# A feed-forward of two matrix products in blocks: written order on four engines, block loads one by one, and the first unit of the second product plain

## The chip, the cores and the metric

One core of a Trainium2 chip runs the kernel. TensorE multiplies (PE; its weight loads are PEld), VectorE works element by element (DVE), ScalarE copies, rounds and applies functions (ACT), GpSimd does a few small powers (POOL), and SyncE (SP) issues the loads from device memory. Each engine runs its own instructions strictly in the order in which they stand on it, and semaphores make one engine wait for another. The metric is the device time of one execution in microseconds (us).

## What is computed

A decoder layer for 256 rows of width 2048, in float32: three attention branches merged by gates, and then a feed-forward block. The change touches the feed-forward alone:

```python
h2 = _rms(x, g_ffn_norm[layer])
x = x + jnp.square(jax.nn.relu(h2 @ w_ff_in[layer])) @ w_ff_out[layer]
```

`w_ff_in` is 2048 x 8192 and `w_ff_out` 8192 x 2048. The kernel takes the 8192 hidden columns in four quarters q of 2048. Quarter by quarter the first product gives the hidden rows, which are squared, turned and kept in `hid`, and the second product adds its part to `x1`.

## The kernel before

**A weight tile.** TensorE multiplies in float32r, so each float32 operand is kept as a rounded part (`hi`) and a remainder (`lo`), and a product takes three passes: hi x hi, lo x hi, hi x lo. A weight tile comes by DMA (`raw`, 128 x 2 x 512), ScalarE casts it to `whi` (L189), and VectorE subtracts to get `wlo` (L190). `raw`, `whi` and `wlo` have four buffers each. `wahead` keeps the two entries behind the current one in preparation, in the order of `plan`.

**Plain strips.** `strip_rows` computes 512 output columns: eight steps of one weight tile, each with 12 matmuls of 128x512 for the two halves of the rows.

**Units.** All but the first quarter's first product goes by `unit`: 1024 columns in which 6 of the 16 row blocks of the weights are multiplied by a Strassen-Winograd scheme with seven products and the other ten steps ("n") are plain tiles. Four weight blocks of 128 x 3 x 512 (B11, B12, B21, B22, tile `sraw`, six buffers) are loaded, and VectorE makes four combinations of them in place or in a fresh buffer: T3 = B22 - B12 in B12's buffer (L211), T2 = B11 + T3 in a new buffer (L213), T1 = B22 - T2 in B11's (L216), T4 = B21 - T2 in T2's (L219). Each of the seven operands is cast and split in two pieces of two and one k-blocks (`SUBS`, written here a and b, as T3a and T3b; lines 263 and 264), with 6 and 3 matmuls. A unit has 10 x 12 + 7 x 9 = 183 matmuls; two plain strips for the same columns have 192. The order of the 24 entries is the list `UNIT`, and `UNIT_LATE` for the first unit of the second product:

```python
UNIT = _order("B11", "T2", "n", "n", "T3", "n", "T1", "n", "B21", "n", "T4", "n", "B22", "n", "n", "n", "n")
```

`early` folds the partial products together after T1 (p1s, uu, wz); `late` takes the finished accumulators of a column half: in the second product an addition to `x1` (L871), in the first product an addition (L846) and two functions on ScalarE (L847, L848), after which `hidden_rows` transposes the rows on TensorE, splits them into `hid`, and for two of the four column groups makes the sums `ss` that the second product's unit needs. These follow-up steps are generators; `pump` advances one step after each entry.

**What sets the order.** The whole program is scheduled when it is built: the code gives priorities, and a scheduler places the instructions of each engine, the DMAs on SP among them. So what stands on an engine can differ from what the code emits.

Of the kernel before, what the change touches and what calls it, by code (L numbers as in the profile page):

```python
# [11 lines left out]
F32 = mybir.dt.float32  # L12
# [42 lines left out]

UNIT = _order("B11", "T2", "n", "n", "T3", "n", "T1", "n", "B21", "n", "T4", "n", "B22", "n", "n", "n", "n")
UNIT_LATE = _order("n", "n", "n", "n", "n", "B11", "T2", "T3", "n", "T1", "n", "B21", "n", "T4", "B22", "n", "n")
UNIT_NORMAL = [(kg, c) for kg in range(SH, KT // GA) for c in range(2)]
# [22 lines left out]

def _units(mat, orders):

    w = mat.reshape(KT, P, -1, 2, 512)
    out = []
    for u, order in enumerate(orders):
        block = lambda kts, c: out.append(np.ascontiguousarray(w[kts, :, u, c].transpose(1, 0, 2)).reshape(-1))
        rest = iter(UNIT_NORMAL)
        for k in order:
            if k == "n":  # L90
                kg, c = next(rest)
                block([GA * kg + g for g in range(GA)], c)
            elif k == ("B11", 0):
                for kts, c in ((K1, 0), (K2, 1), (K1, 1), (K2, 0)):
                    block(kts, c)
    return np.concatenate(out)


@with_exitstack
def tile_block(ctx: ExitStack, tc: tile.TileContext, io):  # L100
# [56 lines left out]
    plan.extend([("w_out", GA, 512)] * (4 * KT // GA))  # L157
    def plan_units(name, orders=(UNIT, UNIT)):
        for order in orders:
            plan.extend((name, GA, 512) if k == "n" else (name, k) for k in order)  # L160

    for q in range(4):
        if q == 0:
            plan.extend([("w_ff_in", GA, 512)] * (4 * KT // GA))
            plan_units("w_ff_out", (UNIT_LATE, UNIT))
        else:
            plan_units("w_ff_in")
            plan_units("w_ff_out")
# [23 lines left out]

    blocks = {}

    def uload(name, which):

        def block():
            off = offs.get(name, 0)
            size = P * SH * 512
            offs[name] = off + size  # L200
            raw = pool[0].tile([P, SH, 512], F32, tag="sraw", name="sraw")
            last_load[0] = nc.sync.dma_start(
                raw, io[name][off:off + size].rearrange("(p g n) -> p g n", p=P, g=SH)).ins
            return raw

        b = blocks
# [61 lines left out]

    def unit(name, sums, xh, xl, early, late, order=UNIT):

# [17 lines left out]

        for what in order:
            if what == "n":  # L290
# [521 lines left out]
    def split_rows():  # L812
        yield
        for g, f in enumerate(scaled):
            yield
            split_into(x1T[:, 4 * g:4 * g + 4, 0, :], x1T[:, 4 * g:4 * g + 4, 1, :], f)
            if g < len(SUBS):
# [3 lines left out]
                        sx[:, :, :, g0:g0 + n, :])  # L821

    for q in range(4):
        hid = [ff.tile([P, 4, 2, S], F32R, tag="hid", name="hid", bufs=4) for _ in range(4)]
# [35 lines left out]
        hidl = lambda kt, t: hid[kt // 4][:, kt % 4, 1, t * P:(t + 1) * P]  # L860
        for u in range(2):
# [12 lines left out]

            unit("w_ff_out", sums_for(lambda kt, hl, ts: hid[kt // 4][:, kt % 4, hl, ts], ss), hidh, hidl, early, late,
                 UNIT_LATE if (q, u) == (0, 0) else UNIT)
        drain(attn, "x")
# [66 lines left out]
```

## Time and profile before

| what | value |
|---|---|
| median of three runs | 1409.28 us (1407.91 to 1409.47) |
| profiled execution: its own time, its span | 1414.6 us, 1412.8 us |
| busy: PE, DVE, ACT | 1394.9, 1039.5, 760.0 us |
| twelve units, second product of q = 0 (u = 1) up to the last unit's start | 526.02 us |
| in these twelve: DVE busy, PE waiting with a named releaser | 473.52 us, 8.2 us |

The profiled execution is 5.3 us above the median of the runs, and its own time is 1.8 us above its span (from the first to the last instruction). PE's busy share says little, since matmuls overlap and their ends are modelled; what tells is the time from one start to the next.

### The profile page before, as it was taken

The page shows a single profiled execution, that of the slowest core. Times are in us where ns is not written, and L with a number is a line of the kernel's source. Part 1 is how long each engine was busy: PE and PEld are TensorE (multiplying, and loading weights), DVE is VectorE, ACT ScalarE, POOL GpSimd, SP SyncE. Part 2 cuts the span into 40 slices and gives each one's busy share as a digit, 9 for nine tenths or more (in the row PEclk, how much of TensorE's full clock was granted, in tenths as well). Part 3 has the DMA queues.
Part 4 walks back from the last instruction along what each step waited for, and adds up shares of the span by engine and source line. Part 5 has one row for each costly group of instructions (what it writes and reads, how often), then busy time and mean ns, then how long its engine had stood idle before and what let it go on. Part 6 is the DMA issues. An engine that isn't in the chain of part 4 may idle for free. (4 is left out here: it accounts for less than half of the span.)

```text
span 1412.8 us, 17222 instructions
## 1 busy us (share of the span) xinstructions
PE 1394.9 (99%) x6334; PEld 1151.0 (81%) x6334; DVE 1039.5 (74%) x1185; ACT 760.0 (54%) x992; POOL 37.6 (3%) x41
## 2 busy tenths in 40 slices
PE   8999999999999999999999999999999999999998
PEld 6888888888888888888888887878888788887887
DVE  6657657566755646565567799988888989888896
ACT  6545545466444444445455655566545665456653
POOL 0211102000000000000000000000000000000000
PEclk9999999999999999999999999999999999999999
DMA  9647545665566666676665746555575555664552
GB/s 324 233 139 240 171 146 165 200 183 164 184 205 199 200 202 200 193 237 201 185 229 183 237 164 228 189 168 179 189 239 191 180 177 191 216 229 151 181 192 90
DMA packets 75236, 274.54 MB, mean 194 GB/s; under 512 B 8592, under 2 KB 9360, under 8 KB 74896
## 3 DMA queue, kind: packets, MB, share of 16 engines
q1 hardware_dynamic: 75008, 273.42, 59.7%
q8 instruction: 50, 0.82, 0.2%
q14 instruction: 34, 0.28, 0.1%
q10 hardware_dynamic: 144, 0.02, 0.0%
HBM read 271.31 MB, written 2.10 MB: 194 GB/s over the span
## 5 line engine op out<-in xcount | busy, mean ns | idle before, releaser
L190 DVE TENSOR_TENSOR wlo<-raw,whi 128x1024 fp32r<-128x1024 f32 (+2 forms) x419 | 501.0, 1204 | 270.6 <-ACT whi L189 260.6
L189 ACT CAST whi<-raw 128x1024 fp32r<-128x1024 f32 (+2 forms) x419 | 432.9, 1038 | 459.4 <-PE acc L253 295.0
L253 PE MATMUL acc<-whi,xT 128*128 128x512 f32 (+1 forms) x1472 | 394.1, 389 | 5.6 <-ACT xT L266 5.6
L253 PEld LDWEIGHTS acc<-whi,xT 128*128 128x128 f32 x1472 | 273.3, 189 | 61.1 <-ACT xT L266 6.3
L253 PE MATMUL acc<-wlo,xT 128*128 128x512 f32 (+1 forms) x736 | 227.1, 389 | 0.0
L263 ACT CAST whi<-sraw 128x1024 fp32r<-128x1024 f32 x196 | 161.8, 837 | 116.1 <-PE acc L280 85.0
L264 DVE TENSOR_TENSOR wlo<-sraw,whi 128x1024 fp32r<-128x1024 f32 x196 | 183.4, 952 | 33.7 <-PE acc L280 19.1
L280 PE MATMUL acc<-whi,hid 128*128 128x512 f32 x736 | 189.7, 390 | 0.0
L280 PEld LDWEIGHTS acc<-whi,hid 128*128 128x128 f32 x736 | 137.5, 188 | 28.2
L253 PEld LDWEIGHTS acc<-wlo,xT 128*128 128x128 f32 x736 | 137.3, 189 | 28.3 <-issue 1.0
L280 PE MATMUL acc<-whi,x1T 128*128 128x512 f32 x552 | 143.6, 396 | 0.0
L280 PEld LDWEIGHTS acc<-whi,x1T 128*128 128x128 f32 x552 | 104.8, 191 | 23.6 <-ACT whi L189 1.6
L280 PE MATMUL acc<-wlo,hid 128*128 128x512 f32 x368 | 102.4, 390 | 0.4 <-DVE wlo L190 0.4
L280 PE MATMUL acc<-wlo,x1T 128*128 128x512 f32 x276 | 77.9, 395 | 5.5 <-DVE wlo L264 5.5
L280 PEld LDWEIGHTS acc<-wlo,hid 128*128 128x128 f32 x368 | 68.7, 188 | 15.9 <-DVE wlo L190 1.8
L253 PE MATMUL acc<-whi,x1T 128*128 128x512 f32 x256 | 70.0, 393 | 0.0
L253 PE MATMUL acc<-whi,mT 128*128 128x512 f32 x256 | 69.9, 391 | 0.0
L280 PEld LDWEIGHTS acc<-wlo,x1T 128*128 128x128 f32 x276 | 51.9, 190 | 18.2 <-DVE wlo L264 6.8
L253 PE MATMUL acc<-whi,oT 128*128 128x512 f32 x224 | 60.0, 390 | 0.6 <-ACT oT L266 0.6
L253 PEld LDWEIGHTS acc<-whi,mT 128*128 128x128 f32 x256 | 47.9, 188 | 9.6
L253 PEld LDWEIGHTS acc<-whi,x1T 128*128 128x128 f32 x256 | 47.5, 188 | 9.4
L253 PEld LDWEIGHTS acc<-whi,oT 128*128 128x128 f32 x224 | 42.0, 188 | 9.5 <-ACT oT L266 0.9
(196 smaller groups left out, 1273.8 us busy)
## 6 DMA issues: line engine op xcount, KB each, us to landing
raw<-in_w_gate_dram SPq DMA_DIRECT2D x96, 512.0 KB, 3.5
raw<-in_w_ff_in_dram SPq DMA_DIRECT2D x92, 512.0 KB, 4.3
raw<-in_w_ff_out_dram SPq DMA_DIRECT2D x80, 512.0 KB, 4.5
raw<-in_w_proj_dram SPq DMA_DIRECT2D x77, 512.0 KB, 3.9
sraw<-in_w_ff_out_dram SPq DMA_DIRECT2D x32, 768.0 KB, 5.4
sraw<-in_w_ff_in_dram SPq DMA_DIRECT2D x24, 768.0 KB, 4.2
raw<-in_w_out_dram SPq DMA_DIRECT2D x32, 512.0 KB, 3.5
raw<-in_w_up_c_dram SPq DMA_DIRECT2D x12, 512.0 KB, 3.5
```

The costliest lines, as they stand in the source:

```text
L189: nc.scalar.copy(hi[:, gs, :], raw[:, gs, :])
L190: nc.vector.tensor_tensor(lo[:, gs, :], raw[:, gs, :], hi[:, gs, :].bitcast(F32), op=ALU.subtract)
L253: nc.tensor.matmul(acc[t][:, :n], lhsT=xs(kt, t), rhs=ws[:, g, :], start=(first and kt == 0), stop=(last and kt == nkt - 1),)
L263: nc.scalar.copy(hi, src)
L264: nc.vector.tensor_tensor(lo, src, hi.bitcast(F32), op=ALU.subtract)
L280: nc.tensor.matmul(acc, lhsT=x(hl, g), rhs=w[:, g, :], start=(first and i == 0 and g == 0), stop=(last and i == 2 and g == n - 1))
```

## The change

1. From the feed-forward on, PE, DVE, ACT and SP keep the order in which the code emits their instructions (`tc.manual_schedule`), where before the scheduler chose it.
2. `UNIT` is reordered: three "n" stand between B11 and T2, T4 goes to the end.
3. The four blocks of the next unit are asked for one at a time, from inside the unit before it (`fetch`): B12 when T2 is made, B11 behind T3's last piece, B21 behind T1's, B22 behind B21's. Before, all four stood at the unit's own start and the scheduler placed them.
4. T4 is made right after B21's last piece.
5. The first unit of the second product (q = 0, columns 0 to 1023) becomes two plain strips.

```diff
-UNIT = _order("B11", "T2", "n", "n", "T3", "n", "T1", "n", "B21", "n", "T4", "n", "B22", "n", "n", "n", "n")
-UNIT_LATE = _order("n", "n", "n", "n", "n", "B11", "T2", "T3", "n", "T1", "n", "B21", "n", "T4", "B22", "n", "n")
+UNIT = _order("B11", "n", "n", "n", "T2", "n", "T3", "n", "T1", "n", "B21", "n", "B22", "n", "T4", "n", "n")
+BLOCKS = {"B12": (0, 1), "B11": (0, 0), "B21": (1, 0), "B22": (1, 1)}
...
+    def fetch(u, n):
+
+        if u == len(units):
+            return
+        name, at = units[u]
+        size = P * SH * 512
+        got = ready.setdefault(u, {})
+        for i, k in enumerate(list(BLOCKS)[len(got):n], len(got)):
+            off = (at * len(BLOCKS) + i) * size
+            got[k] = pool[0].tile([P, SH, 512], F32, tag="sraw", name="sraw")
+            last_load[0] = nc.sync.dma_start(
+                got[k], io[name][off:off + size].rearrange("(p g n) -> p g n", p=P, g=SH)).ins
...
         if which == ("B11", 0):
-            b.update({k: block() for k in ("B11", "B22", "B12", "B21")})
+            fetch(u, len(BLOCKS))
+            b.update(ready.pop(u))
         elif which == ("T2", 0):
             b["T3"] = b.pop("B12")
             nc.vector.tensor_tensor(b["T3"], b["B22"], b["T3"], op=ALU.subtract)
             b["T2"] = pool[0].tile([P, SH, 512], F32, tag="sraw", name="sraw")
             nc.vector.tensor_tensor(b["T2"], b["B11"], b["T3"], op=ALU.add)
+            fetch(u + 1, 1)
         elif which == ("T1", 0):
             b["T1"] = b.pop("B11")
             nc.vector.tensor_tensor(b["T1"], b["B22"], b["T2"], op=ALU.subtract)
-        elif which == ("T4", 0):
-            b["T4"] = b.pop("T2")
-            nc.vector.tensor_tensor(b["T4"], b["B21"], b["T4"], op=ALU.subtract)
         g0, n = SUBS[which[1]]
         hi = wp.tile([P, n, 512], F32R, tag="whi", name="whi")
         lo = wp.tile([P, n, 512], F32R, tag="wlo", name="wlo")
-        split_into(hi, lo, b[which[0]][:, g0:g0 + n])
+        split_into(hi, lo, b[k][:, g0:g0 + n])
+        if last:
+            if k == "B21":
+                b["T4"] = b.pop("T2")
+                nc.vector.tensor_tensor(b["T4"], b["B21"], b["T4"], op=ALU.subtract)
+            if k in ("T3", "T1", "B21"):
+                fetch(u + 1, {"T3": 2, "T1": 3, "B21": 4}[k])
+            if k == "T4":
+                done[0] += 1
+                b.clear()
         return hi, lo
...
+    ET = mybir.EngineType
+    ctx.enter_context(tc.manual_schedule(engines={ET.PE, ET.DVE, ET.Activation, ET.SP}))
     for q in range(4):
...
+        for c in range(0 if q else 2):
+            acc = strip_rows("w_ff_out", 512, KT, hidh, hidl)
+            cs = slice(c * 512, (c + 1) * 512)
+            for t in range(2):
+                nc.vector.tensor_tensor(x1[:, t, cs], acc[t], x1[:, t, cs], op=ALU.add)
+        for u in range(0 if q else 1, 2):
```

**SP, the loads of one unit** (first product, q = 1, u = 0), before: `sraw` are blocks of the next unit, `raw` the tiles of the "n" entries, in the queue's order. The `sraw` rows are B11, B22 and B12 of the next unit; in the built program the second waits until VectorE has split T3b, the third until it has split T1b.

```order
L202 DMA sraw_8844<-in_w_ff_in_dram 128x1536
L186 DMA raw_8578<-in_w_ff_in_dram 128x1024
L186 DMA raw_8591<-in_w_ff_in_dram 128x1024
L186 DMA raw_8636<-in_w_ff_in_dram 128x1024
L186 DMA raw_8673<-in_w_ff_in_dram 128x1024
L186 DMA raw_8716<-in_w_ff_in_dram 128x1024
L186 DMA raw_8752<-in_w_ff_in_dram 128x1024
L202 DMA sraw_8846<-in_w_ff_in_dram 128x1536
L186 DMA raw_8787<-in_w_ff_in_dram 128x1024
L202 DMA sraw_8848<-in_w_ff_in_dram 128x1536
```

The same unit in the change; here `sraw_8566`, `8626`, `8665` and `8711` are B12, B11, B21 and B22 of the next unit.

```order
L184 DMA raw_8521<-in_w_ff_in_dram 128x1024
L184 DMA raw_8534<-in_w_ff_in_dram 128x1024
L184 DMA raw_8543<-in_w_ff_in_dram 128x1024
L203 DMA sraw_8566<-in_w_ff_in_blocks_dram 128x1536
L184 DMA raw_8602<-in_w_ff_in_dram 128x1024
L203 DMA sraw_8626<-in_w_ff_in_blocks_dram 128x1536
L184 DMA raw_8640<-in_w_ff_in_dram 128x1024
L203 DMA sraw_8665<-in_w_ff_in_blocks_dram 128x1536
L184 DMA raw_8679<-in_w_ff_in_dram 128x1024
L203 DMA sraw_8711<-in_w_ff_in_blocks_dram 128x1536
L184 DMA raw_8725<-in_w_ff_in_dram 128x1024
```

Before, six tiles stood ahead of the first block that waits for T3b, of which two are used by then. Now four stand ahead of it, and all four are used by then: the fifth tile, `raw_8640`, has moved behind the block. In the built program `sraw_8626` waits for VectorE's split `wlo_8623` (T3b), `sraw_8665` for `wlo_8662` (T1b), and `sraw_8711` for the combination that writes `sraw_8564` (T4); the `raw` rows behind them need no buffer that is not long free.

**DVE, the same unit in the change**, from T3's last piece on (`sraw_8227` is T3, `sraw_8287` T1, `sraw_8326` B21, `sraw_8564` T4).

```order
L276 TENSOR_TENSOR wlo_8623<-sraw_8227,whi_8622 128x512
L188 TENSOR_TENSOR wlo_8642<-raw_8640,whi_8641 128x1024
L222 TENSOR_TENSOR sraw_8287<-sraw_8375,sraw_8564 128x1536
L276 TENSOR_TENSOR wlo_8655<-sraw_8287,whi_8654 128x1024
L276 TENSOR_TENSOR wlo_8662<-sraw_8287,whi_8661 128x512
L188 TENSOR_TENSOR wlo_8681<-raw_8679,whi_8680 128x1024
L276 TENSOR_TENSOR wlo_8693<-sraw_8326,whi_8692 128x1024
L780 TENSOR_TENSOR uu_8700<-pp_8608,p1s_8699 128x512
L781 TENSOR_TENSOR uu_8700<-pp_8646,uu_8700 128x512
L782 TENSOR_TENSOR wz_8701<-pp_8685,uu_8700 128x1024
L276 TENSOR_TENSOR wlo_8707<-sraw_8326,whi_8706 128x512
L230 TENSOR_TENSOR sraw_8564<-sraw_8326,sraw_8564 128x1536
```

The next row is the split of `raw_8725`. So each of the three tiles is needed by the very instruction that follows the one its load waits for; before, four tiles lay between.

**ACT at the end of that unit**, before: `y_8872` belongs to the first column half, `y_8892` and `y_8896` are the second's; `raw_8928` and `raw_8948` the first two "n" tiles of the next unit.

```order
L848 ACTIVATE y_8872<-y_8872 128x512
L847 ACTIVATE y_8892<-y_8892 128x512
L189 CAST whi_8929<-raw_8928 128x1024
L847 ACTIVATE y_8896<-y_8896 128x512
L189 CAST whi_8949<-raw_8948 128x1024
L848 ACTIVATE y_8892<-y_8892 128x512
```

In the change (`y_8856` and `y_8860` are the second half's, `raw_8864` and `raw_8877` are the first two tiles of the next unit):

```order
L275 CAST whi_8840<-sraw_8626 128x512
L861 ACTIVATE y_8856<-y_8856 128x512
L862 ACTIVATE y_8856<-y_8856 128x512
L861 ACTIVATE y_8860<-y_8860 128x512
L862 ACTIVATE y_8860<-y_8860 128x512
L187 CAST whi_8865<-raw_8864 128x1024
L187 CAST whi_8878<-raw_8877 128x1024
```

The casts of the next unit's first tiles have moved behind all the functions of the last column half.

## Rows read from the trace of the kernel before

**Rows 1.** The page: span; busy us of each engine (share, instructions).

```profile
span 1412.8 us, 17222 instructions
...
PE 1394.9 (99%) x6334; PEld 1151.0 (81%) x6334; DVE 1039.5 (74%) x1185; ACT 760.0 (54%) x992; POOL 37.6 (3%) x41
```

**Rows 2.** Windows cut at the units' starts: length, busy PE, PEld, DVE, ACT, POOL, PEclk.

```profile
927.40:975.82 48.42, 45.82 (x201) 36.95 (x200) 41.90 (x50) 29.43 (x41) 0.00 (x0) 0.96 0.52 174
975.82:1019.14 43.32, 43.32 (x200) 35.96 (x199) 39.58 (x42) 27.46 (x37) 0.00 (x0) 1.00 0.58 194
1019.14:1060.65 41.51, 41.51 (x184) 34.28 (x183) 37.85 (x39) 22.06 (x26) 0.00 (x0) 1.00 0.60 203
...
sum 526.02, PE 517.85 PEld 424.44 DVE 473.52 ACT 308.04 POOL 0.00; mean PE 43.15 PEld 35.37 DVE 39.46 ACT 25.67 POOL 0.00
```

**Rows 3.** Waits of PE in the twelve units: total us, times, longest.

```profile
PE acc L280 <- DVE wlo L264: 5.5, 3, 2.2
PE pp L280 <- DVE sf L752: 2.3, 3, 0.8
```

**Rows 4.** DVE's groups in the twelve units: busy us, mean ns | idle before.

```profile
L190 DVE TENSOR_TENSOR wlo<-raw,whi 128x1024 fp32r<-128x1024 f32 x121 | 144.5, 1219 | 10.7 <-ACT whi L189 4.5 <-ACT whi L263 4.1 <-issue 1.7
...
L264 DVE TENSOR_TENSOR wlo<-sraw,whi 128x512 fp32r<-128x512 f32 x85 | 58.3, 686 | 21.3 <-PE acc L280 12.3 <-PE pp L280 8.1
...
L211 DVE TENSOR_TENSOR sraw<-sraw 128x1536 f32<-128x1536 f32 x12 | 21.1, 1756 | 6.8 <-DMA sraw<-in_w_ff_out_dram 4.3 <-DMA sraw<-in_w_ff_in_dram 2.5
...
L871 DVE TENSOR_TENSOR x<-acc,x 128x512 f32<-128x512 f32 x26 | 16.7, 682 | 0.0
...
L749 DVE TENSOR_TENSOR sf<-tp,a21s 128x256 f32<-128x256 f32 x3 | 1.3, 417 | 0.0
```

**Rows 5.** Timeline of DVE: start, us; two splits that follow each other.

```profile
1029.20 1.21 DVE L190 TENSOR_TENSOR wlo<-raw,whi 128x1024 fp32r<-128x1024 f32 x1
1030.33 1.22 DVE L264 TENSOR_TENSOR wlo<-sraw,whi 128x1024 fp32r<-128x1024 f32 x1
```

**Rows 6.** ACT's groups in the twelve units, columns as in rows 4.

```profile
L189 ACT CAST whi<-raw 128x1024 fp32r<-128x1024 f32 x120 | 124.6, 1052 | 103.3 <-PE acc L280 63.6 <-PE pp L280 20.4 <-issue 9.0
...
L263 ACT CAST whi<-sraw 128x512 fp32r<-128x512 f32 x85 | 52.8, 621 | 51.7 <-PE acc L280 29.3 <-DVE x L871 18.1 <-DVE wlo L264 2.9
L847 ACT ACTIVATE y<-y 128x512 f32<-128x512 f32 x24 | 15.0, 629 | 5.3 <-DVE y L846 5.3
...
L263 ACT CAST hid<-tp 128x512 fp32r<-128x512 f32 x24 | 13.7, 583 | 6.7 <-PE tp L782 6.7
```

**Rows 7.** Waits of SP's queue in the twelve units: total us, times, longest.

```profile
SPq L186 <- DVE wlo L190: 312.7, 118, 11.3
SPq L202 <- DVE wlo L264: 124.9, 44, 5.6
```

**Rows 8.** Timeline of SP: a block and a tile issued one after the other.

```profile
1033.73 0.33 SPq L202 DMA_DIRECT2D sraw<-in_w_ff_in_dram  x1
1034.93 0.33 SPq L186 DMA_DIRECT2D raw<-in_w_ff_out_dram  x1
```

**Rows 9.** The same two in the view of DMAs: KB, us from issue to landing.

```profile
sraw<-in_w_ff_in_dram SPq DMA_DIRECT2D x1, 768.0 KB, 4.1
raw<-in_w_ff_out_dram SPq DMA_DIRECT2D x1, 512.0 KB, 4.6
```

**Rows 10.** The tile `raw` on SP in the twelve units, 121 loads.

```profile
DMA to landing us min/median/max: 3.4/4.6/7.0
```

**Rows 11.** Timeline of PE after a wait [idle before <- releaser].

```profile
1299.00 1.22 PE L280 MATMUL acc<-wlo,x1T 128*128 128x512 f32 x2 [2.19 <-DVE wlo L264]
1300.02 2.54 PE L280 MATMUL acc<-whi,x1T 128*128 128x512 f32 x6
```

**Rows 12.** Two windows behind that wait, columns as in rows 2.

```profile
1299.00:1302.00 3.00, 3.00 (x7) 2.42 (x8) 2.77 (x5) 2.06 (x3) 0.00 (x0) 0.50 0.22 39
1302.00:1306.00 4.00, 4.00 (x18) 3.23 (x18) 2.94 (x5) 1.82 (x4) 0.00 (x0) 0.98 0.75 301
```

More of the change, by code (lines that the diff above doesn't have):

```diff
@@ L79, in _blocked, with _unit_rest, _unit_blocks @@
     return np.concatenate(out)
[L82 to L96, printed above, removed]
+def _unit_rest(mat):
+    w = mat.reshape(KT // GA, GA, P, -1, 2, 512).transpose(3, 0, 4, 2, 1, 5)
+    return np.concatenate([u[kg, c].reshape(-1) for u in w for kg, c in UNIT_NORMAL])
+def _unit_blocks(mat):
+    w = mat.reshape(KT, P, -1, 2, 512).transpose(2, 3, 1, 0, 4)
+    return np.concatenate([u[c][:, (K1, K2)[h]].reshape(-1) for u in w for h, c in BLOCKS.values()])
 @with_exitstack
@@ L157, in tile_block, with plan_units @@
     plan.extend([("w_out", GA, 512)] * (4 * KT // GA))
-    def plan_units(name, orders=(UNIT, UNIT)):
-        for order in orders:
-            plan.extend((name, GA, 512) if k == "n" else (name, k) for k in order)
+    units = []
+    def plan_units(name, count=2):
+        for _ in range(count):
+            units.append((name + "_blocks", sum(n == name + "_blocks" for n, _ in units)))
+            plan.extend((name, GA, 512) if k == "n" else (name, k) for k in UNIT)
     for q in range(4):
         if q == 0:
-            plan.extend([("w_ff_in", GA, 512)] * (4 * KT // GA))
-            plan_units("w_ff_out", (UNIT_LATE, UNIT))
+            plan.extend([("w_ff_in", GA, 512)] * (4 * KT // GA) + [("w_ff_out", GA, 512)] * (2 * KT // GA))
+            plan_units("w_ff_out", 1)
         else:
@@ L191, in wload @@
         return hi, lo
-    blocks = {}
-    def uload(name, which):
[L197 to L206, printed above, removed]
+    blocks, ready, done = {}, {}, [0]
+    def fetch(u, n):
[9 more added lines that the diff above has]
+                got[k], io[name][off:off + size].rearrange("(p g n) -> p g n", p=P, g=SH)).ins
+    def uload(name, which):
+        b, u = blocks, done[0]
+        k, last = which[0], which[1] == len(SUBS) - 1
         if which == ("B11", 0):
-            b.update({k: block() for k in ("B11", "B22", "B12", "B21")})
+            fetch(u, len(BLOCKS))
+            b.update(ready.pop(u))
         elif which == ("T2", 0):
@@ L267, in split_into, with unit @@
             nc.vector.scalar_tensor_tensor(lo, src, scale, hi.bitcast(F32), op0=ALU.mult, op1=ALU.subtract)
-    def unit(name, sums, xh, xl, early, late, order=UNIT):
+    def unit(name, sums, xh, xl, early, late):
         bank, r = {}, {}
@@ L287, in rest @@
             return r[c, t], fresh
-        for what in order:
+        for what in UNIT:
             if what == "n":
@@ L860, in tile_block @@
         hidl = lambda kt, t: hid[kt // 4][:, kt % 4, 1, t * P:(t + 1) * P]
-        for u in range(2):
+        for c in range(0 if q else 2):
[4 more added lines that the diff above has]
+        for u in range(0 if q else 1, 2):
             cols = [slice(1024 * u + 512 * c, 1024 * u + 512 * (c + 1)) for c in range(2)]
@@ L873, in late @@
                     load(io["out"][t * P:(t + 1) * P, cols[c]], x1[:, t, cols[c]])
-            unit("w_ff_out", sums_for(lambda kt, hl, ts: hid[kt // 4][:, kt % 4, hl, ts], ss), hidh, hidl, early, late,
-                 UNIT_LATE if (q, u) == (0, 0) else UNIT)
+            unit("w_ff_out", sums_for(lambda kt, hl, ts: hid[kt // 4][:, kt % 4, hl, ts], ss), hidh, hidl, early, late)
         drain(attn, "x")
@@ L931 @@
         "w_ff_in": np.concatenate(
-            [_blocked(a["w_ff_in"][0][:, :DM], COL_STRIPS, GA), _units(a["w_ff_in"][0][:, DM:], [UNIT] * 6)]),
-        "w_ff_out": np.concatenate([_units(a["w_ff_out"][0][q * DM:(q + 1) * DM], [UNIT if q else UNIT_LATE, UNIT]) for q in range(4)]),
+            [_blocked(a["w_ff_in"][0][:, :DM], COL_STRIPS, GA), _unit_rest(a["w_ff_in"][0][:, DM:])]),
+        "w_ff_in_blocks": _unit_blocks(a["w_ff_in"][0][:, DM:]),
+        "w_ff_out": np.concatenate(
+            [_blocked(a["w_ff_out"][0][:DM, :1024], COL_STRIPS[:2], GA), _unit_rest(a["w_ff_out"][0][:DM, 1024:])]
+            + [_unit_rest(a["w_ff_out"][0][q * DM:(q + 1) * DM]) for q in range(1, 4)]),
+        "w_ff_out_blocks": np.concatenate(
+            [_unit_blocks(a["w_ff_out"][0][q * DM:(q + 1) * DM, 0 if q else 1024:]) for q in range(4)]),
     }
```

## The prediction

> **What bounds the kernel now.** First the page: of the span [rows 1] the last half is the feed-forward, and the change leaves the instructions ahead of it as they are. So I went to the units, cut at their starts. Twelve of them take 526.0 us, and VectorE is busy for 473.5 us of it, 90% [rows 2]. A unit that waits for nothing takes 41.5 us, which for 183 matmuls is 0.227 us each, and 43.3 us where transposes of the hidden rows fall into it; the expensive ones are the three second units of the first product, 48.4 us in the row shown [rows 2]. Transposes fall into every other unit, so TensorE's work alone is 42.4 us on average, 509 us for twelve, and some 17 us are waits and what follows them. The list of waits names 5.5 us for a late split and 2.3 us for the sums [rows 3]. Behind it stands a DMA: T3's combination waited 6.8 us in all for its block to land [rows 4]. So TensorE bounds the units, with VectorE close behind. VectorE has some 4.4 us to spare in a unit, (526.0 - 473.5) / 12; what makes it idle for longer becomes time.
>
> The second thing to see is SP. It waits for 118 tiles and 44 blocks until VectorE has released a buffer [rows 7]; a waiting load holds up all that stands behind it in the queue. Before, the tiles do not suffer from it, since each is asked for when the tile four places ahead of it is done.
>
> **What the change removes.** The blocks are asked for much earlier, so the 6.8 us of waits for blocks go, and with them most of the 17 us. That is the gain, at most 17 us.
>
> **What it adds, small.** The plain strips have 192 - 183 = 9 matmuls more: 9 x 0.227 = 2.0 us on TensorE, since nothing else there hides it. VectorE gets shorter there, which buys nothing: TensorE bounds that stretch.
>
> **What it adds, large: three late tiles per unit.** When T2 is made, B12 of the next unit takes the sixth and last `sraw` buffer. B11 of the next unit then needs T3's buffer, so its load waits on SP until VectorE has split T3b. Behind it in the queue stands the tile that VectorE needs in its very next instruction, as the listings of SP and VectorE show. The same happens behind T1b and behind T4's combination. Before, four tiles were in stock at that place; now none is. So at each of the three places VectorE and ScalarE have nothing they may do until the tile has landed and been cast.
>
> How long is that? No row shows a tile issued directly behind a released block. The nearest: a block and then a tile 1.20 us later, the block landing after 4.1 us and the tile after 4.6 [rows 8, 9], which is 1.20 + 4.6 = 5.8 us after the block was issued. I take 5.8. From below, the tile lands like a lone one: 0.33 us of issue [rows 8] and 3.4 us [rows 10], 3.7 us. From above, like the slowest: 0.33 + 7.0 = 7.3 us [rows 8, 10]. With the cast of 1.05 us [rows 6] and three hand-overs of about 0.03 us, VectorE stands still for 6.93 us each time.
>
> The Trainium skill, DMA: Bandwidth & Descriptors, section "Anatomy of one DMA — SWDGE (gpsimd) path", gives 2.0 us and bytes / 436 GB/s for a load issued by GpSimd; for the block and the tile as one (1.31 MB) an estimate by that page is 5.0 us, and the sum below would be 36 x 0.8 = 29 us less. The trace does not agree on such a pair, 5.8 us with the tile issued 1.2 us late, and the sum goes by the trace.
>
> **One unit, walked.** Splits of VectorE that follow each other start 1.13 us apart, for a duration of 1.21 [rows 5]. So I count 1.13 for a full split, 0.60 for a half (0.68 less the same 0.08), 1.67 for a combination; the last before another engine takes over counts in full [rows 4]. Zero is the end of T3b's split.
>
> *From zero to the tile behind T4.* First wait 6.93. Then its split 1.13, T1's combination 1.76, the cast of T1a 1.05 with hand-overs 1.12, split T1a 1.13, T1b 0.69: 12.8. Second wait: 19.7. Then a tile 1.13, B21a 1.13, `early` 0.60 + 0.60 + 1.13, B21b 0.60, T4's combination 1.76: 26.6. In the second product `early` also adds to `x1`, 0.60 + 0.60 + 1.13, so 29.0. Third wait, until TensorE can start: 33.6 in the first product, 35.9 in the second.
>
> *From there to the unit's end* TensorE has 4 x 12 + 2 x 9 = 66 matmuls, 15.0 us, and it starts at half clock. After a wait of 2.19 us the trace shows seven matmuls in 3 us at a granted clock of 0.50, the 1.2 GHz level, and then 0.98 [rows 11, 12]. Eight or nine at twice the time cost 1.7 us; 16.7 us in all. The same restart behind the first two waits lies inside the next wait and costs nothing.
>
> *From the unit's end to the next zero*, VectorE again, since the three tiles, T2 and T3 of the next unit stand behind `late` in its order. After a unit of the second product: last addition 0.64, three tiles 3.39, two combinations 3.43, cast of T2a 1.12, then T2a, T2b, a tile, T3a, T3b 1.13 + 0.60 + 1.13 + 1.13 + 0.69: 13.3 us. After one of the first product the next unit's tiles are cast behind the four functions of the last half, 0.63 us each [rows 6]. The last addition ends at 1.8, since it stands behind B11b's split, which waits for the first half's functions; two functions and a cast later, at 4.1, the first tile is there. Then come its split, a tile, half a `hid`, a tile (1.13 + 1.13 + 0.60 + 1.13, at 8.1), the other half of `hid`, whose transposes stand on TensorE behind that first tile (8.8), two combinations 3.43, the cast 1.12, and T2a, T2b, a tile, `hid`, T3a, `hid`, T3b with 1.13 + 0.60 + 1.13 + 0.60 + 1.13 + 0.60 + 0.69: 19.3 us. Where the first sums stand in the row as well, four operations of 0.41 us [rows 4], a cast and a split add 3.8: 23.1 us.
>
> Zero to zero: 35.9 + 16.7 + 13.3 = 65.9 us for the six of the second product; 33.6 + 16.7 + 19.3 = 69.6 and 33.6 + 16.7 + 23.1 = 73.4 for three each of the first. The last unit asks for nothing and keeps its length. Twelve: 395.4 + 208.8 + 220.2 = 824 us, against 526 [rows 2]: 298 us more. The check: VectorE's work per unit is about 40 us, three waits of 6.9 make 61, and the rest is the time in which it waits for TensorE at the unit's end.
>
> **The sum.** Span 1412.8 [rows 1] + 298 + 2.0 = 1713 us; own time 1.8 more, 1715; the median lay 5.3 us below the profiled execution's own time, so 1709.
>
> **Rivals.**
>
> *The tiles land like lone ones.* 3.7 us instead of 5.8, 36 times: 76 us less, 1633 us. For it: the tile is issued right behind the block, not 1.2 us later. Against: the block's 768 KB go first, and the pair shown took 5.8 us [rows 8, 9].
>
> *The queue does not bind, the hand-over does.* If tiles were in time, TensorE would still wait behind first-product units: 1.6 us for the first tile (4.1 less 2.0 of B11's matmuls and 0.5 of transposes), 0.8 for its split and T2a's, and 3.7 more for T2b where the sums stand ahead of it. That is 3 x 2.4 + 3 x 6.1 us and some four restarts of 1.7, 32 us; less the 17 that go, plus 2.0: 1426 us. For it: ScalarE's order as listed. Against: the loads' order.
>
> *Faster.* Neither binds: 1409 - 17 + 2 = 1394 us. It decides where the three waits together fall under VectorE's 4.4 us to spare, some 1.5 us each: a tile would have to be issued 5.5 us ahead of T3b's end. Against: the order gives it no lead at all.
>
> *The clock stays low.* If TensorE ran at the low level through all 66 matmuls, that would be 13.2 instead of 1.7 us more: 138 us, 1847 us. Against: it came back after 3 us in the row [rows 12]. The Trainium skill, TensorE: Matmul & The Clock Gate, section "HAM oscillation — how this bites in real kernels", tells of a kernel that waits for DMA between its bursts of matmuls and starts every burst at the low clock. By that rule the price is one restart for each wait, as walked; the trace agrees for its one long wait [rows 11], and no run here shows a row of them.
>
> **How the numbers follow.** The forecast as walked, roughly 1660 to 1780, has 0.74; lone landing 0.10; hand-over only 0.06; faster 0.04; clock stays low 0.06. The prediction is the walked sum, 1709 us. The range goes from the lone landing, 1633, to the slowest landing (1.5 us more, 36 times: 54 us, 1763) with some room for the walk: 1630 to 1780, which leaves 0.16 out. A measurement here tells 0.2% (2.8 us) from no change. Slower takes the forecast, lone landing, hand-over and clock, 0.95 with a little taken off for the hand-over's size; faster 0.04; the same 0.01.
>
> **What would show it.** Right: the list of waits has ScalarE's cast of `raw` waiting for the DMA some 36 times, about 5.8 us each, and VectorE's split behind it; VectorE's busy time stays near 1030 us while its share falls to about 60%; TensorE waits for casts in each unit in three or four places of 2 to 9 us, and its granted clock falls to half behind them; unit starts 65 to 74 us apart. Wrong: if those casts wait less than 4 us each, my landing time is off; if SP issues the tile ahead of T3b's end, the mechanism is; if units are 42 to 45 us apart with waits only behind the functions, the hand-over rival holds.

## The result and the profile after

The changed kernel takes 1746.68 us (median of 4 runs, 1743.25 to 1747.71), beside 1408.6 us for the kernel before on the same chip: 1.240 times as long (95% interval 1.238 to 1.242), 338 us more. The forecast was 1709 us in a range of 1630 to 1780.

The page of the changed kernel, its span and the busy time of each engine:

```profile
span 1744.6 us, 17105 instructions
...
PE 1499.2 (86%) x6343; PEld 1208.1 (69%) x6343; DVE 1034.1 (59%) x1167; ACT 752.7 (43%) x983; POOL 36.6 (2%) x41
```

Beside [rows 1]: VectorE and ScalarE do the same work, in a longer span. Now one cut into three: up to the first unit, the twelve units, and the last unit with the end (length, busy PE, PEld, DVE, ACT, POOL, PEclk, DMA share, GB/s). First and third window of the kernel before (its twelve units are the sum in [rows 2]):

```profile
0.00:841.49 841.49, 835.37 (x3852) 692.44 (x3852) 533.11 (x653) 432.77 (x586) 37.58 (x41) 1.00 0.63 199
...
1367.51:1412.80 45.29, 41.64 (x184) 34.17 (x182) 32.91 (x36) 19.17 (x22) 0.00 (x0) 0.98 0.35 117
```

The same three windows of the changed kernel:

```profile
0.00:847.99 847.99, 840.01 (x3868) 694.46 (x3869) 517.70 (x638) 425.89 (x576) 36.63 (x41) 1.00 0.63 197
847.99:1687.49 839.50, 613.78 (x2293) 477.64 (x2292) 478.66 (x492) 306.25 (x384) 0.00 (x0) 0.85 0.33 120
1687.49:1744.60 57.11, 45.43 (x184) 36.03 (x182) 37.79 (x37) 20.53 (x23) 0.00 (x0) 0.94 0.36 120
```

The stretch up to the first unit is 6.5 us longer, the twelve units 313.5 us (839.50 - 526.02), the last unit and the end 11.8 us. So the place is the one that was forecast: VectorE is busy for 479 us of the twelve units as before, but that is now 57% of them, and the granted clock of TensorE is 0.85 on average. Four units in a row of the changed kernel (second product of q = 1, u = 0 and 1, then first product of q = 2, u = 0 and 1), same columns:

```profile
1055.42:1127.79 72.37, 51.63 (x201) 40.02 (x199) 42.47 (x44) 27.13 (x36) 0.00 (x0) 0.86 0.32 116
1127.79:1194.69 66.90, 49.23 (x184) 38.74 (x183) 38.79 (x38) 21.64 (x26) 0.00 (x0) 0.85 0.35 126
1194.69:1259.37 64.68, 48.42 (x184) 38.22 (x183) 35.16 (x33) 22.84 (x28) 0.00 (x0) 0.87 0.36 130
1259.37:1335.23 75.86, 54.86 (x200) 42.03 (x199) 43.06 (x49) 30.51 (x42) 0.00 (x0) 0.84 0.31 111
```

Every unit is 65 to 76 us long, where [rows 2] has 41.5 to 48.4. What VectorE does inside one, from T3's last piece on, shows the timeline of DVE (start, us, and in brackets the idle time before and who ended it):

```profile
860.69 1.82 DVE L276 TENSOR_TENSOR wlo<-sraw,whi 128x1024 fp32r<-128x1024 f32 x2
869.11 1.23 DVE L188 TENSOR_TENSOR wlo<-raw,whi 128x1024 fp32r<-128x1024 f32 x1 [6.61 <-ACT whi L187]
870.26 1.75 DVE L222 TENSOR_TENSOR sraw<-sraw 128x1536 f32<-128x1536 f32 x1
873.20 1.83 DVE L276 TENSOR_TENSOR wlo<-sraw,whi 128x1024 fp32r<-128x1024 f32 x2 [1.19 <-ACT whi L275]
881.57 1.23 DVE L188 TENSOR_TENSOR wlo<-raw,whi 128x1024 fp32r<-128x1024 f32 x1 [6.54 <-ACT whi L187]
```

T3b's split ends at 862.51, and the split of the tile behind it waits 6.61 us for ScalarE's cast; behind T1b it is 6.54 us. The cast is not the cause, it waits itself. SP in the same stretch:

```profile
862.53 0.33 SPq L203 DMA_DIRECT2D sraw<-in_w_ff_in_blocks_dram  x1
862.95 0.38 SPq L184 DMA_DIRECT2D raw<-in_w_ff_out_dram  x1
```

The block goes out 0.02 us after T3b's split ended, and the tile 0.42 us behind the block. The view of DMAs for that tile (KB, us to landing), beside [rows 9]:

```profile
raw<-in_w_ff_out_dram SPq DMA_DIRECT2D x1, 512.0 KB, 5.0
```

So the tile is there 0.42 + 5.0 = 5.4 us after the block's issue; in the 36 pairs of block and tile of the trace it is 5.3 to 5.6 us. The third place, behind T4's combination, has a wait of 6.68 us. Over the twelve units the groups of DVE and ACT that answer to [rows 4] and [rows 6] (busy us, mean ns | idle us before, and what ended it):

```profile
L188 DVE TENSOR_TENSOR wlo<-raw,whi 128x1024 fp32r<-128x1024 f32 x120 | 145.3, 1222 | 271.8 <-ACT whi L187 271.8
```

```profile
L187 ACT CAST whi<-raw 128x1024 fp32r<-128x1024 f32 x120 | 125.1, 1047 | 347.9 <-DMA raw<-in_w_ff_out_dram 166.8 <-DMA raw<-in_w_ff_in_dram 141.2 <-PE acc L292 38.0
```

The durations are those of before; the idle time ahead of VectorE's splits of tiles has gone from 10.7 to 271.8 us, and ahead of ScalarE's casts it is now mostly the DMA that ends it. The list of PE's waits in the twelve units, beside [rows 3] (total, times, longest):

```profile
PE acc L292 <- ACT whi L187: 211.7, 42, 7.8
```

### The profile page after: what moved, and what is told of

The parts are those of the page before. It is cut to its first block, busy times and chain, and to the rows that moved or that the text cites. A ratio compares the mean times of both kernels' runs of the same rounds, so it can differ in the third digit from the quotient of the medians.

```text
span 1744.6 us, 17105 instructions
## 1 busy us (share of the span) xinstructions
PE 1499.2 (86%) x6343; PEld 1208.1 (69%) x6343; DVE 1034.1 (59%) x1167; ACT 752.7 (43%) x983; POOL 36.6 (2%) x41
## 5 line engine op out<-in xcount | busy, mean ns | idle before, releaser
L188 DVE TENSOR_TENSOR wlo<-raw,whi 128x1024 fp32r<-128x1024 f32 (+2 forms) x425 | 509.7, 1205 | 545.9 <-ACT whi L187 540.5
L187 ACT CAST whi<-raw 128x1024 fp32r<-128x1024 f32 (+2 forms) x425 | 438.4, 1036 | 684.4 <-PE acc L265 272.2
L292 PE MATMUL acc<-whi,hid 128*128 128x512 f32 x644 | 206.6, 447 | 115.8 <-ACT whi L187 115.8
L292 PE MATMUL acc<-whi,x1T 128*128 128x512 f32 x552 | 184.7, 463 | 101.4 <-ACT whi L187 101.4
L292 PEld LDWEIGHTS acc<-whi,x1T 128*128 128x128 f32 x552 | 123.2, 228 | 136.8 <-ACT whi L187 109.7
L275 ACT CAST whi<-sraw 128x1024 fp32r<-128x1024 f32 (+1 forms) x182 | 146.9, 832 | 150.3 <-DVE sraw L218 63.5
L276 DVE TENSOR_TENSOR wlo<-sraw,whi 128x1024 fp32r<-128x1024 f32 (+1 forms) x182 | 169.0, 954 | 67.2 <-ACT whi L275 65.5
L292 PE MATMUL acc<-wlo,hid 128*128 128x512 f32 x322 | 113.6, 434 | 7.0 <-DVE wlo L276 5.5
L292 PE MATMUL acc<-wlo,x1T 128*128 128x512 f32 x276 | 99.8, 444 | 0.2
L292 PEld LDWEIGHTS acc<-wlo,x1T 128*128 128x128 f32 x276 | 60.9, 222 | 16.3 <-DVE wlo L188 2.0
L265 PE MATMUL acc<-whi,x1T 128*128 128x512 f32 x256 | 69.8, 393 | 0.0
L265 PEld LDWEIGHTS acc<-whi,x1T 128*128 128x128 f32 x256 | 47.5, 188 | 9.5
```

Of the source, the lines that this page charges most:

```text
L187: nc.scalar.copy(hi[:, gs, :], raw[:, gs, :])
L188: nc.vector.tensor_tensor(lo[:, gs, :], raw[:, gs, :], hi[:, gs, :].bitcast(F32), op=ALU.subtract)
L265: nc.tensor.matmul(acc[t][:, :n], lhsT=xs(kt, t), rhs=ws[:, g, :], start=(first and kt == 0), stop=(last and kt == nkt - 1),)
L275: nc.scalar.copy(hi, src)
L276: nc.vector.tensor_tensor(lo, src, hi.bitcast(F32), op=ALU.subtract)
L292: nc.tensor.matmul(acc, lhsT=x(hl, g), rhs=w[:, g, :], start=(first and i == 0 and g == 0), stop=(last and i == 2 and g == n - 1))
```

## The experiments

Twelve kernels. All but e8 start from the changed kernel. The last column is the median less that of the kernel before on the same chip.

| run | what it is | median us | over before |
|---|---|---|---|
| | changed kernel | 1746.7 | +338 |
| e1 | three blocks one tile later on SP | 1522.0 | +113 |
| e2 | one of the three blocks later | 1678.3 | +269 |
| e3 | blocks at their own unit's start | 1500.5 | +92 |
| e4 | SP scheduled; PE, DVE, ACT written | 1489.3 | +80 |
| e5 | all engines scheduled | 1410.4 | 0 |
| e6 | SP written; PE, DVE, ACT scheduled | 1570.3 | +160 |
| e7 | stores on another queue | 1739.7 | +329 |
| e8 | kernel before, first unit plain | 1411.8 | +1 |
| e9 | seven buffers instead of six | 1508.9 | +100 |
| e10 | only ACT written | 1442.5 | +34 |
| e11 | only DVE written | 1452.2 | +43 |
| e12 | scheduled, seven buffers, stores moved | 1414.3 | +5 |

**e1, the blocks one tile later.** A block that falls due is held back until the next tile's load has been issued.

```diff
@@ wload, behind the tile's dma_start
+        if owed_[0]:
+            owed_[0]()
@@ uload
-                fetch(u + 1, {"T3": 2, "T1": 3, "B21": 4}[k])
+                owed.append([1 if k in ('T3', 'T1', 'B21') else 0, u + 1, {"T3": 2, "T1": 3, "B21": 4}[k]])
+                pay()
```

> The same program as the changed kernel, but each of the three blocks that a unit asks for on behalf of the next one stands on SP's queue one ordinary tile further back, so that the tile needed next is asked for ahead of the block that waits for its buffer. Theory (the tile behind the waiting block lands late, three times in each of twelve units, 6.6 us of VectorE wait each): most of the 338 us goes; what is left is the tile behind, late by an estimated 0.8 us at the second place and 3.5 us at the third, so 1420 to 1465 us. Rival (functions and casts standing in written order on ScalarE and VectorE make the time, not the loads): still 1650 us or more. Rival (the blocks' bytes beside the tiles' make the tiles slow): about 1740 us, since the same bytes move.

Measured 1522.0 us. 225 of the 338 us go with three loads moved by one place each, so the rivals fall; but 57 us more are left than the theory's upper end. VectorE's wait for casts of tiles from the first unit to the end, first in the changed kernel, then in e1:

```profile
DVE wlo L188 <- ACT whi L187: 280.8, 71, 6.9
DVE wlo L191 <- ACT whi L190: 64.5, 30, 7.2
```

Of the 113 us left a part is still late tiles: at the third place VectorE stands still for 3.7 to 3.9 us in each of the twelve units, as the expectation had it (3.5). In the first unit:

```profile
885.58 1.23 DVE L191 TENSOR_TENSOR wlo<-raw,whi 128x1024 fp32r<-128x1024 f32 x1 [3.76 <-ACT whi L190]
```

The larger part, which the theory did not have, is not at these places; e4 shows it.

**e2, one of the three.** The same edit for T3 alone (`1 if k in ('T3',) else 0`).

> The same move for one of the three blocks only, the one asked for behind T3's last piece. Theory: one of the three waits of 6.6 us goes in each of twelve units, 79 us, so about 1668 us (1655 to 1690), as three times this saving is what the first run shows. Rival (whichever place waits, the next place takes the wait over, since the engines are short of lead in the whole unit): within 20 us of 1747. Rival (a single place is the root and the others follow from it): near the time of the kernel with all three moved.

Measured 1678.3 us, 68.4 less than the changed kernel, 5.7 us for each of twelve places; three times that is 205, near e1's 225. VectorE's wait for casts of tiles, over the same stretch as in e1, is 72 us shorter than in the changed kernel (280.8 - 208.8):

```profile
DVE wlo L191 <- ACT whi L190: 208.8, 62, 6.9
```

The places pay one by one; neither does the next one take the wait over, nor is one of them the root.

**e3, the blocks at their own start.**

```diff
-            fetch(u + 1, 1)
...
-            if k in ("T3", "T1", "B21"):
-                fetch(u + 1, {"T3": 2, "T1": 3, "B21": 4}[k])
```

> No block is asked for inside the unit before; all four are asked for together at the head of their own unit, two entries ahead of its first piece, as the kernel before does; the order of the tiles inside a unit, the in-order queues and the plain first unit stay. Theory: none of the four buffers is still in use at that point, so no tile stands behind a waiting block; what is left is the start of a unit, where the first piece waits for its block, at most 2 to 4 us for each of twelve units: 1425 to 1470 us. Rival (written order on four engines): 1600 us or more, since that order is kept.

Measured 1500.5 us: part 3 of the change, undone alone, gives back 246 us, but 30 us less than the theory's range wanted. As in e1, something besides the late tiles is left.

**e4 to e6, who keeps the written order.** Only the set in `manual_schedule` differs: e4 without SP, e5 without any engine, e6 with SP alone.

```diff
-    ctx.enter_context(tc.manual_schedule(engines={ET.PE, ET.DVE, ET.Activation, ET.SP}))
+    ctx.enter_context(tc.manual_schedule(engines={ET.PE, ET.DVE, ET.Activation}))
```

> The changed kernel with SP's own order given back to the scheduler, PE, VectorE and ScalarE still in written order; the scheduler then puts about six more tiles ahead of the blocks in the first units of the feed-forward, but in the later ones still single tiles between blocks. Theory: a block holds up a tile only where the tile stands behind it and is needed within about 5 us of the block's release; by the order listing the later units keep one tile between two blocks, so part of the waits stays: 1450 to 1650 us, with the rows of the waits showing VectorE's wait only where a tile stands right behind a block. Rival (written order on PE, VectorE, ScalarE is the cause): 1700 us or more.

> The changed kernel without the written order on any engine; the blocks asked for one by one and the plain first unit stay. The run with SP alone given back stands at 1489, with waits of PE for ScalarE's and VectorE's casts of about 6 us in each of two units out of four, at the places where one unit is handed to the next. Theory (what is left there is the written order on ScalarE and VectorE, functions of the old unit ahead of casts of the new): these waits go and the time falls by 75 to 85 us to 1400 to 1418. Rival (the blocks asked for one by one cost something by themselves, whoever sets the order): 1440 to 1490.

> Written order on SP alone; PE, VectorE and ScalarE go back to the scheduler. Theory (the late tiles are SP's doing and add to the hand-over, which is the other engines'): 1747 less about 80, so 1650 to 1690. Rival (the two costs are one and the same, each hides behind the other): within 20 us of 1747. Rival (written order on SP costs only together with written casts, since a scheduler that puts other work ahead of a late cast hides it): under 1550.

Measured 1489.3, 1410.4 (ratio to before 1.0007, 0.9998 to 1.0016) and 1570.3 us. The windows of the twelve units, e4:

```profile
848.14:1436.43 588.29, 541.97 (x2293) 429.61 (x2292) 475.41 (x492) 308.79 (x385) 0.00 (x0) 0.97 0.52 173
```

e5:

```profile
845.01:1365.33 520.32, 513.98 (x2289) 424.59 (x2288) 466.00 (x488) 312.94 (x385) 0.00 (x0) 0.99 0.60 192
```

e6:

```profile
844.09:1518.11 674.02, 558.13 (x2293) 447.70 (x2292) 474.35 (x491) 302.45 (x383) 0.00 (x0) 0.93 0.41 146
```

So the four cases are 0 with no written order, 80 with it on PE, VectorE and ScalarE, 160 on SP alone, 338 on all: the two parts cost 240 by themselves and 98 more together. e6's rivals both fall: late tiles cost without written casts, and they cost less than with them. But its theory, a plain sum with 1650 to 1690 us, was missed too, by 80 us. The granted clock of the four windows of twelve units (0.99, 0.97, 0.93 and, in the changed kernel, 0.85) goes the same way. Estimated from these rows, the time lost at the low level, (1 - clock) x length, is 5, 18, 47 and 126 us, so at most 66 of the 98 us are the clock's (126 - 18 - 47 + 5); it counts stretches in which TensorE waits too, and how the 98 divide is not shown. PE's waits from the first unit to the end in e6 name the same place as in the changed kernel, 35 times, 3.3 us each instead of 5.0:

```profile
PE acc L292 <- ACT whi L187: 116.2, 35, 5.9
```

Why the scheduled engines lose less at each late tile is open; the row says how much, not what they did meanwhile. e4's 80 us are another matter. That a part of the late tiles would stay in e4 was wrong: no cast of a tile waits for a DMA in its twelve units (group of ACT, columns as above):

```profile
L187 ACT CAST whi<-raw 128x1024 fp32r<-128x1024 f32 x121 | 126.6, 1051 | 61.8 <-PE acc L292 42.5 <-DVE wlo L276 13.2 <-PE pp L292 4.5
```

Its timeline of ACT, from the end of a unit of the first product:

```profile
994.83 0.63 ACT L862 ACTIVATE y<-y 128x512 f32<-128x512 f32 x1
995.36 1.98 ACT L187 CAST whi<-raw 128x1024 fp32r<-128x1024 f32 x2
```

The cast of the new unit's first tile follows the last of the old unit's four functions without a wait: it is ScalarE's order that it waits for, not its load. In the next unit, e4's timeline of DVE has the additions to `x1` ahead of B21b's split, and PE waits for that split:

```profile
1023.93 1.22 DVE L887 TENSOR_TENSOR x<-wz,x 128x1024 f32<-128x1024 f32 x1
1025.06 0.68 DVE L276 TENSOR_TENSOR wlo<-sraw,whi 128x512 fp32r<-128x512 f32 x1
```

```profile
1025.80 0.50 PE L292 MATMUL acc<-wlo,hid 128*128 128x512 f32 x1 [2.39 <-DVE wlo L276]
```

**e7, the stores.**

```diff
-                    load(io["out"][t * P:(t + 1) * P, cols[c]], x1[:, t, cols[c]])
+                    nc.gpsimd.dma_start(io["out"][t * P:(t + 1) * P, cols[c]], x1[:, t, cols[c]])
```

> The changed kernel with the eight stores of the output put on GpSimd's queue in place of SP's, so that the last unit's tiles do not stand behind stores that wait for additions. Theory (the stores cost the last two units what the forecast left out, about 7.6 us ahead of the last unit's start and 3.4 us in its tail): 7 to 11 us less, 1736 to 1740. Rival (the last unit is long for another reason, its functions or its order): within 2 us of 1747.

Measured 1739.7 us, 6.9 less, or 9 by the last column (329 instead of 338), so about what was expected. In the changed kernel SP has the four stores of the last but one unit, which wait for the additions to `x1`, ahead of the last unit's tiles (timeline of SP), and PE then waits for the first of them (timeline of PE):

```profile
1684.33 4.41 SPq L241 DMA_DIRECT2D out_dram<-x  x4
1688.84 1.35 SPq L184 DMA_DIRECT2D raw<-in_w_ff_out_dram  x3
```

```profile
1695.23 2.08 PE L292 MATMUL acc<-whi,hid 128*128 128x512 f32 x4 [5.53 <-ACT whi L187]
```

With the stores elsewhere the last window is 49.7 instead of 57.1 us, and the granted clock stays at 1.00 in it:

```profile
1687.47:1737.20 49.73, 42.25 (x184) 34.02 (x182) 37.33 (x37) 19.14 (x22) 3.07 (x6) 1.00 0.28 97
```

**e8, the plain first unit alone.** The kernel before with this one part.

```diff
-            plan.extend([("w_ff_in", GA, 512)] * (4 * KT // GA))
-            plan_units("w_ff_out", (UNIT_LATE, UNIT))
+            plan.extend([("w_ff_in", GA, 512)] * (4 * KT // GA) + [("w_ff_out", GA, 512)] * (2 * KT // GA))
+            plan_units("w_ff_out", (UNIT,))
```

> The kernel before with one part of the change alone: the first unit of the second product computed plain, 9 matmuls more and no sums for it; order and loads otherwise as before. By the forecast 2.0 us more, so 1410.6, within 0.2 per cent (1408 to 1413). Rival (the waits of before at that unit's start go with it): 2 to 6 us faster, 1403 to 1407. Rival (a new wait at the hand-over from the plain strips to the first unit): 1415 or more.

Measured 1411.75 beside 1410.56 us (ratio 1.0008, 0.9998 to 1.0017): 1.2 us more, which holds both the 2.0 of the sum and nothing; the rivals are out.

**e9, a seventh buffer.** Order and loads stay as in the changed kernel. The edits left out make room: two small tables move into attention's pool, and a tile that is only a filler goes.

```diff
-    wff = ctx.enter_context(tc.tile_pool(name="wff", bufs=6, side="right"))
+    wff = ctx.enter_context(tc.tile_pool(name="wff", bufs=7, side="right"))
...
-    rrow = ff.tile([P, S], F32, name="rrow")
+    rrow = ff.tile([P, 512], F32, tag="p1", name="rrow", bufs=1)[:, :S]
```

> The changed kernel, written order on all four engines and the loads where they stand, with a seventh buffer for blocks and combinations in place of six (room for it is made by two small tables that live only as long as attention, and by one row buffer that shares another's place). The block asked for behind T3's, T1's and B21's last piece then takes a buffer whose last reader is done some 20 us earlier, so no block stands waiting on SP's queue. Theory (a tile is late because the block ahead of it waits for its buffer): all 36 late tiles go and the kernel stands where the runs without them stand, 1480 to 1510. Rival (the tiles are late because a block's bytes go ahead of theirs): 1700 or more, since the order on the queue is the same.

Measured 1508.9 us: 237.8 us less than the changed kernel, close to 36 x 6.6. The twelve units:

```profile
848.09:1447.70 599.61, 546.87 (x2294) 431.49 (x2292) 476.06 (x492) 305.99 (x384) 0.00 (x0) 0.96 0.46 168
```

The wording was wrong in one thing. A block still stands on SP until T3b's split is done (here at 1015.66), as the timeline of SP of e9 shows:

```profile
1015.68 0.33 SPq L201 DMA_DIRECT2D sraw<-in_w_ff_out_blocks_dram  x1
1016.06 0.42 SPq L182 DMA_DIRECT2D raw<-in_w_ff_out_dram  x1
```

But with one buffer more it is the next block, which stands one tile further back, and the tile behind it is needed one place later. The timeline of DVE of e9 from T3's last piece on (a tile's split; then, left out, T1's combination and its pieces; the next tile):

```profile
1015.57 1.22 DVE L186 TENSOR_TENSOR wlo<-raw,whi 128x1024 fp32r<-128x1024 f32 x1
...
1022.29 1.22 DVE L186 TENSOR_TENSOR wlo<-raw,whi 128x1024 fp32r<-128x1024 f32 x1 [0.81 <-ACT whi L185]
```

The first tile waits for nothing now, and the second 0.81 us instead of 6.54. The bytes and their order are the same, so the rival falls.

**e10 and e11, which of the engines.** `{ET.Activation}` and `{ET.DVE}` as the only member of the set.

> Written order on ScalarE alone, the other engines scheduled (1410 with none written; 1489 with PE, VectorE and ScalarE written). Theory (at the hand-over of a unit ScalarE's functions of the old unit stand ahead of its casts of the new one): most of the 79 us is here, 1450 to 1490. Rival (VectorE's order, its additions ahead of its low parts): 1408 to 1425 here.

> Written order on VectorE alone, the other engines scheduled. Theory (the price is ScalarE's): 1408 to 1430. Rival (VectorE's additions and sums ahead of the low parts of the next tiles): 1450 to 1490. If both of these runs stay under 1430, the price needs the two orders together.

Measured 1442.5 us (34 over before), between the two ranges, and 1452.2 us (43 over before), in the rival's range: VectorE's order has a price of its own. The two add up to 77, and e4 with both and PE has 80; PE's order alone was not run. So the hand-over's price comes from ScalarE's order and VectorE's, about half each. In e11 PE's longest waits are not for splits behind additions, but for casts of the combinations' pieces:

```profile
PE pp L292 <- ACT whi L275: 14.6, 9, 1.7
```

Which of VectorE's instructions of the old unit makes the 43 us is therefore not shown.

**e12, a try for the best.** Seven buffers, no written order, stores on GpSimd's queue.

> A try for a version that beats both: no written order, seven buffers, blocks asked for one by one, the first unit plain, the output's stores on GpSimd's queue. With no written order PE waits 6.3 us in the feed-forward by the run before, all for sums on VectorE, and none for loads; what a seventh buffer and other stores can give is then the tail, 0 to 5 us: 1404 to 1411. Rival (the schedule shifts and a new wait appears): over 1413.

Measured 1414.3 us beside 1408.9 (ratio 1.0023, 1.0010 to 1.0036): over the 1404 to 1411 that were expected, and in the rival's range. No version here beats the kernel before; the best of the changed ones, e5, equals it. In e5 PE waits for nothing but the sums, 6.3 us where [rows 3] has 2.3 and another 5.5 for a late split:

```profile
PE pp L292 <- DVE sf L761: 6.3, 3, 2.1
```

e12 has the same 6.3 us; where its 5 us lie is open.

## Why the prediction was right, and where it missed

**The gain, at most 17 us.** No run shows it. Without a written order (e5) the twelve units take 520.3 instead of 526.0 us, each from one profiled execution. But e8, which asks for the blocks as before, has 519.4:

```profile
844.53:1363.97 519.44, 513.62 (x2293) 420.92 (x2292) 466.75 (x490) 307.41 (x385) 0.00 (x0) 1.00 0.58 193
```

And in e5 T3's combination waits longer for its block than the 6.8 us of [rows 4]:

```profile
L216 DVE TENSOR_TENSOR sraw<-sraw 128x1536 f32<-128x1536 f32 x12 | 21.1, 1758 | 15.2 <-DMA sraw<-in_w_ff_in_blocks_dram 10.3 <-DMA sraw<-in_w_ff_out_blocks_dram 4.8
```

So these waits do not set the time of the units there, the step from the 6.8 us to most of the 17 is not borne out, and e5 as a whole equals the kernel before. In the changed kernel the same group waits 0.0 us, but what that gave cannot be told apart from the loss. The walked sum did not use the gain, so it stands without it.

**Three late tiles per unit.** Right, and shown: with the tile one place ahead (e1) or one buffer more (e9), most of VectorE's waits go. The landing was 5.4 us behind the block's issue, not 5.8: the tile left 0.42 us behind the block and not 1.20, and took 5.0 instead of 4.6. The Trainium skill's formula (DMA: Bandwidth & Descriptors, section "Anatomy of one DMA — SWDGE (gpsimd) path") is for loads that GpSimd issues; the forecast's estimate by it for such a pair, 5.0 us, was as far below the trace as the forecast was above it. That 5.8 was so near is partly luck: the pair of [rows 8, 9] is nearly the shortest of 18 such pairs of the kernel before, which have 5.8 to 6.8 us, 6.1 in the middle. VectorE stood still for 6.5 to 6.9 us at 33 of the 36 places, forecast 6.93, and for 4.3 at three, where the sums filled 2.3 us of the wait; 232 us together (250 at the forecast's size). e9 gave back 237.8, but that it is so near to 36 x 6.6 is chance: in e9's twelve units VectorE's waits for casts of tiles are 225.8 us shorter (271.8 - 46.0), the units 239.9. The sign that was named, casts that wait for the DMA 36 times for 5.8 us, read 38 times and 8.1 us (308.0 in all), since ScalarE was done with T3's casts 1.8 us before the block went out (860.72 and 862.53).

**The walk of a unit.** From zero to TensorE's start behind T4 33.2 and 35.4 us (forecast 33.6 and 35.9) in the timelines, from there to the unit's end 16.5 to 17.9 (16.7), from there to the next zero 13.6 behind the second product, 20.5 behind the first and 25.5 with the sums in it (13.3, 19.3, 23.1). That start in the changed kernel:

```profile
897.89 2.08 PE L292 MATMUL acc<-whi,hid 128*128 128x512 f32 x4 [7.81 <-ACT whi L187]
```

and two windows behind it, beside [rows 12]:

```profile
897.80:900.80 3.00, 2.91 (x7) 2.33 (x8) 2.93 (x4) 2.45 (x4) 0.00 (x0) 0.50 0.92 321
900.80:915.22 14.42, 14.42 (x61) 11.80 (x60) 9.35 (x11) 6.66 (x8) 0.00 (x0) 0.93 0.56 193
```

One restart at the low level behind this wait, as walked. The rival of a clock that stays low would have 28 us from each such start to the unit's end (16.7 + 11.5), where all twelve have 16.5 to 17.9, so it falls. The four units shown above take 279.8 us, walked 274.8 (2 x 65.9 + 69.6 + 73.4): 5 us too few, three times. By e9 the late tiles are 240 of the 313.5 us (839.5 - 599.6), for which the walk had 250; the other 74, which e9 keeps, had 48. The step that was sized too small is above all the stretch from the unit's end to the next zero, 4.2 us in four units, mostly where the sums stand in it: the next unit's casts and splits behind functions, sums and additions. The run of TensorE to the unit's end was 2.4 us too short as well, and the way to its start 1.7 too long.

**"The last unit asks for nothing and keeps its length."** Wrong. It asks for no block, but its tiles stand on SP behind stores that wait: 11.8 us more with the end, of which e7 takes back 7.4. The walk had counted the loads that stand behind a waiting load, and not those behind stores, which share the queue.

**The stretch up to the first unit.** Forecast +2.0, measured +6.5; in e8's profile it is +3.0 (844.53), though its median is only 1.2 over before. The full +6.5 is there in e4 too (848.14) and not in e5 (845.01), so about 3 us of it belong to the written order on PE, VectorE and ScalarE.

**The sum.** Span 1712.8 forecast, 1744.6 measured: 15.5 us in the twelve units, 11.8 in the last, 4.5 ahead of the first. The other 5.6 us up to the median are the assumption that it lies below the profiled execution, as before; it lay 2.1 above the span.

**The hand-over rival** was named with 1426 us, 32 us gross. Its mechanism is in the chain, beside the late tiles and not in their place; by itself it makes 80 us (e4), not 32. The forecast counted waits behind first-product units alone. The additions of the second product ahead of B21b's split (2.39 us of PE above) were in the walk of VectorE, but not in the rival; and some waits cost more at the low clock than the 1.7 us taken. In e4, PE's timeline has a wait of 1.88 us with four transposes ahead of it:

```profile
955.23 1.22 PE L292 MATMUL pp<-whi,sx 128*128 128x512 f32 x2 [1.88 <-ACT whi L275]
```

and the windows from there on (PEclk stands behind the busy times):

```profile
955.00:957.80 2.80, 2.45 (x7) 1.56 (x8) 2.80 (x4) 2.56 (x4) 0.00 (x0) 0.51 0.00 0
957.80:961.80 4.00, 4.00 (x11) 3.17 (x11) 3.67 (x8) 1.64 (x4) 0.00 (x0) 0.50 0.60 151
```

Here the 1.2 GHz level holds for 6.6 us (955.23 to 961.80). Not every wait has such a price: over e4's twelve units the clock is 0.97, an estimated 18 of the 62 us that they are longer than before (588.3 - 526.0), and PE's listed waits add up to 45 us, beside 8.2.

**Lone landing, faster.** Both out: the tile landed at 5.4 us, and its load never stood ahead of T3b's end.

## What to carry to other kernels

On a queue that issues in order, look at what stands behind each transfer that waits for its buffer, stores included, and at how soon it is needed; one place in the order (e1) or one buffer (e9) was worth 225 to 238 us here. A written order on the engines that prepare operands has a price where one stage hands over to the next: without late loads it still cost 80 us, half on ScalarE and half on VectorE. The timelines show the next stage's casts and splits behind the last stage's functions and additions; no run here tried a better written order, and the scheduler's costs nothing (e5). And price a rival by itself before giving it a small chance: two causes that both held cost 98 us more together than apart.

## What was not expected of the hardware

That a tile goes out sooner behind its block changed little in its own landing. In the changed kernel's 36 pairs, 0.37 to 0.42 us apart, the tile took 4.9 to 5.2 us. In the 18 pairs of the kernel before that are 1.13 to 1.34 us apart, it took 4.5 to 5.7; another of them than that of [rows 9], issued at 1008.82:

```profile
raw<-in_w_ff_out_dram SPq DMA_DIRECT2D x1, 512.0 KB, 5.0
```

And the granted clock fell to 0.50 behind waits of TensorE of only 1.9 to 2.4 us, for some 3 us in [rows 12] and 6.6 in e4, but not behind each of them. A later unit of e4 has waits of up to 2.2 and 1.9 us at the same places and keeps the high level throughout (PEclk stands behind the busy times):

```profile
1131.72:1186.99 55.27, 47.01 (x200) 35.14 (x199) 42.84 (x49) 30.54 (x42) 0.00 (x0) 1.00 0.46 153
```

So what a wait of that length costs has to be read from its own rows.
